# Message passing on sorted edges: register loads once per run, ahead of the clearing matmul

## The chip, the cores and the metric

The kernel runs on one core of one Trainium2 chip. The metric is the device time of one execution in microseconds. The time before the change is 506.3 us, the median of three executions (505.32 to 507.6).

## The reference

4096 nodes have 256 features each, and 262,144 edges have a source and a destination, drawn at random. Each edge carries its source's features, transformed, to its destination, where the messages are summed:

```python
self_out = nodes @ w_self
src_feat = nodes[edges_src]
msg = src_feat @ w_msg
agg = np.zeros((N, D), dtype=np.float32)
np.add.at(agg, edges_dst, msg)
return (self_out + agg).astype(np.float32)
```

## The kernel before

The kernel turns the gather and the scatter into matmuls. In the first 193 us it sorts the edges on VectorE (DVE), with transposes on TensorE (PE), by a key of three parts: a segment of 374 destinations (SW; there are 11, NSEG), a block of 128 sources (NB = 32), and the destination. It also projects all nodes, Y = nodes @ w_msg, in 32 blocks. The sorted edges are cut into 2048 chunks (NCOL) of 128.

The stage after the sort, the run stage, is what the change touches. A run is one pair of segment and source block; there are 11 x 32 = 352 (NRUN), with 5.8 chunks on average. For each run PE builds a matrix of edge counts, 128 sources by 374 destinations plus a spill of 112, in one of six PSUM banks (RING). In program order, the loop over the chunks (lines 422 to 450) does this:

- DVE builds one-hot matrices for 32 chunks at a time, `e` (source within its block) and `d` (destination relative to the chunk's smallest), in four buffers each (line 312).
- `clear(r)` (343 to 350) is a matmul with zeros that opens run r's bank: 224 columns, the two strips where runs overlap. It waits for the eviction of run r - 6, which had the same bank. It is issued nine chunks (MARG) before the run's expected first chunk, `first(r)`.
- For each chunk one matmul (`count_mm`, line 440) adds the one-hot product, 112 columns wide, to the ring at an offset that depends on the data. The offset was computed on DVE into the tile `poff`, 128 rows of 16 values (G16). [...] it must be loaded from `poff` by PE's own instruction stream (lines 430 to 432, eight chunks at a time).
- `evac(r)` (352 to 362): when nine chunks past the run's expected end are done, ScalarE (ACT) copies the bank to SBUF as bf16, into one of 14 buffers of `atr`.
- `merge` (369 to 376): for two of three pairs of runs the spill columns are added into the next run's buffer by an accumulating DMA that GpSimd (POOL) issues. For the others PE does it, with one more matmul (392).
- `apply_run` (378 to 410): some 46 chunks later (LAG), PE multiplies the counts with Y in three matmuls of 256 columns (397) into `out_ps`. At the first run of a segment six matmuls (386) put in nodes @ w_self; at its last, ACT copies the result out and SyncE (SP) stores it.

The order on every engine is the one written here (`manual_schedule`): no scheduler moves anything. Each matmul on PE is two instructions, a weight load (LDWEIGHTS, PEld in the profile) and the matmul proper. The compiled order puts the weight load of the first matmul after a register load ahead of that register load. So before the change the sequence is LDWEIGHTS of a chunk, register load, matmul of that chunk. A wait on another engine sits on the weight load.

Of the kernel before, what the change touches and what calls it, by code (L numbers as in the profile page):

```python
# [20 lines left out]
BW = 512  # L21
SW = 374
W = 112
# [4 lines left out]
RING = 6  # L28
MARG = 9
# [5 lines left out]
PSUM0 = 0x2000000  # L35
# [32 lines left out]
def kernel(  # L68
# [9 lines left out]
    nc = tc.nc  # L78
# [4 lines left out]
    NCOL = E // P  # L83
    assert NCOL == 2048
    T = N // P
    G16 = NCOL // P
# [77 lines left out]
    for h in range(NQ):  # L164
# [3 lines left out]
        c = slice(h * HC, (h + 1) * HC)  # L168
# [24 lines left out]
    end = (NRUN - 1) * SW + N - (NSEG - 1) * SW - SW * OFF  # L193
# [37 lines left out]
    def col16(name, dt):  # L231
        return meta.tile([P, G16], dt, name=name)

    k16, kn, g7f = (col16(n, FP32) for n in ("k16", "kn", "g7f"))
    k16i, kni, rho, rhoc, gi, g7, gn, dl, sl, wr, poff = (
        col16(n, I32)
        for n in ("k16i", "kni", "rho", "rhoc", "gi", "g7", "gn", "dl", "sl", "wr", "poff")
    )
# [66 lines left out]
    def onehots(c, n):  # L305
        res = []
        if c in split_at:
            split_vals(c, split_at[c])
        for nm, val, wid in (("e", slo_b, P), ("d", rel_b, W)):
            o = ohp.tile([P, 16, wid, 2], BF16, name=nm + "_oh", tag=nm, bufs=4)  # L310
            shp = [P, n // 2, wid, 2]
            tt(  # L312
                out=o[:, 0:n // 2],
                in0=val[:, c:c + n].rearrange("p (g i) -> p g i", i=2).unsqueeze(2).to_broadcast(shp),
                in1=jrow[:, 0:wid, :].unsqueeze(1).to_broadcast(shp),
                op=ALU.is_equal,
            )
            res.append(o)
        return res


    def first(r):
        return 187 * r // 32 if r <= NRUN - NB else 1870 + 89 * (r - NRUN + NB) // 16
# [6 lines left out]
    def count_mm(ap, lhsT, rhs, start, after=()):  # L330
        mm = nc.tensor.matmul(  # L331
            out=ap, lhsT=lhsT, rhs=rhs, start=start, stop=True, skip_group_check=True,
        ).ins
        tc.declare_no_dep(
            mm, group="evac", keep=after, reason="disjoint banks by static schedule"
        )
        for i in after:
            tc.add_manual_dep(mm, i.name, DEP, reason="bank free")
        tc.add_to_no_dep_group("count", mm)
        last_mm[0] = mm  # L340
        return mm

    def clear(r):
        b = (r % RING) * BW
        after = [evac_of[r - RING]] if r >= RING else []
        zone = bass.AP(
            tensor=ring.tensor, offset=ring[:, b:b + 1].offset,
            ap=[list(ring[:].ap[0]), [SW, 2], [1, W]],
        )
        count_mm(zone, zer[:, 0, :], zer[:, 1:3, 0:W], True, after)  # L350

    def evac(r):
        at = ats[r % NAT]
        b = (r % RING) * BW
        ins = nc.scalar.copy(out=at[:, 0:SW + W], in_=ring[:, b:b + SW + W]).ins  # L355
        tc.declare_no_dep(
            ins, group="count", keep=[last_mm[0]], reason="disjoint banks by static schedule"
        )
        tc.add_manual_dep(ins, last_mm[0].name, DEP, reason="run complete")
        tc.add_to_no_dep_group("evac", ins)  # L360
        evac_of[r] = ins
        at_of[r] = at
# [3 lines left out]
    def by_dma(r):  # L366
        return r < NRUN - 8 and r // 2 % 3 > 0

    def merge(r):

        i, j = r % NAT, (r + 1) % NAT
        pairs = [(i, j, 2)] if j + 2 <= NAT else [(i, j, 1), (j, 0, 1)]
        for a, b, n in pairs:
            nc.gpsimd.dma_start(  # L374
                out=atr[:, b:b + n, 0:W], in_=atr[:, a:a + n, SW:SW + W], accum_op=ALU.add
            )

    def apply_run(r):
        s, b = divmod(r, NB)
        at = at_of[r]  # L380
        if b == 0:
            for t in range(NT):
                c0 = s * SW + t * P
                m = min(P, N - c0)
                for k in range(2):
                    nc.tensor.matmul(  # L386
                        out=out_ps[0:m, t, :], lhsT=XT[:, k, c0:c0 + m], rhs=wcat[:, k, :],
                        start=(k == 0 and t % 2 == 0), stop=False, skip_group_check=True,
                    )
        spill = at_of.pop(r - 1, None)  # L390
        if r > 0 and not by_dma(r - 1):
            nc.tensor.matmul(  # L392
                out=out_ps[:, 0, :], lhsT=spill[:, SW:SW + P], rhs=Y[:, b, :],
                start=False, stop=False, skip_group_check=True,
            )
        for t in range(NT):
            nc.tensor.matmul(  # L397
                out=out_ps[:, t, :], lhsT=at[:, t * P:(t + 1) * P], rhs=Y[:, b, :],
                start=False, stop=(b == NB - 1), skip_group_check=True,
            )  # L400
        if b == NB - 1:
            o_sb = ohp.tile([P, 3, D], FP32, name="o_sb", tag="o_sb", bufs=2)
            r0, r1 = s * SW, min(s * SW + SW, N)
            nc.scalar.copy(out=o_sb[:, 0:2, :], in_=out_ps[:, 0:2, :])  # L404
            nc.sync.dma_start(
                out[r0:r0 + 2 * P, :].rearrange("(t p) f -> p t f", p=P), o_sb[:, 0:2, :]
            )
            m = r1 - r0 - 2 * P
            nc.scalar.copy(out=o_sb[0:m, 2, :], in_=out_ps[0:m, 2, :])  # L409
            nc.sync.dma_start(out[r0 + 2 * P:r1, :], o_sb[0:m, 2, :])  # L410

    if True:
        todo = []
        regs = []
        ncl = 0
        nev = 0
        starts = {}
        c = 0
        for n in sizes:
            starts[c] = n  # L420
            c += n
        for c in range(NCOL):
            if c in starts:
                c0 = c
                e, d = onehots(c, starts[c])
            ci = c - c0
            while ncl < NRUN and first(ncl) - MARG <= c:
                clear(ncl)
                ncl += 1
            if c % 8 == 0:  # L430
                regs = [nc.tensor.alloc_register(f"po{c}_{i}") for i in range(8)]
                nc.tensor.load(regs, poff[c // G16:c // G16 + 1, c % G16:c % G16 + 8])
            addr = nc.tensor.snap(
                regs[c % 8], donate=True, min_val=PSUM0, max_val=PSUM0 + 4 * (RING * BW - W)
            ).with_bounds(
                min_val=PSUM0, max_val=PSUM0 + 4 * (RING * BW - W),
                guaranteed_mod_val=0, out_of_modulus=4,
            )
            off = (addr - PSUM0) // 4
            count_mm(  # L440
                ring[:, bass.ds(off, W)], e[:, ci // 2, :, ci % 2], d[:, ci // 2, :, ci % 2], False
            )
            while nev < NRUN and (first(nev + 1) - 1 + MARG <= c or c == NCOL - 1):
                evac(nev)
                if nev % 2 == 0 and nev and by_dma(nev - 1):
                    merge(nev - 2)
                todo.append((c + LAG + (SWITCH if nev % NB == 0 else 0), nev))
                nev += 1
            while todo and (todo[0][0] <= c or c == NCOL - 1):
                apply_run(todo.pop(0)[1])  # L450
# [344 lines left out]
```

## Time and profile before

| | |
|---|---|
| median of three executions | 506.3 us |
| the profiled execution, its own time | 506.48 us |
| its span, first to last instruction | 504.5 us |
| PE, DVE, ACT, POOL busy | 355.6, 447.4, 237.9, 158.6 us |
| first and last register load from poff | 194.9 and 492.0 us |
| register loads from poff, of eight registers each | 256 |
| mean granted TensorE clock | 0.916 |

The page cuts the span into 40 slices of 12.6 us and gives each engine's busy share in each, in tenths; the run stage is slices 15 to 39. Each of the costliest groups of instructions has a line: source line, engine, operation, tiles, count, then busy time in all, mean length of one in ns, and the idle time of the engine just before them with what ended most of it. "issue" is a wait that ends with nothing that the profile shows. A matmul's recorded length (213 ns for a chunk) is longer than its distance from the next (51 ns), since matmuls are pipelined. Register loads are not counted as busy; they appear only in the view of their tile or line, under PE's sequencer (PEldq).

### The profile page before, as it was taken

How to read it: one execution, taken by the hardware profiler on the slowest of the kernel's cores; microseconds unless marked ns; L12 is line 12 of the kernel's file. 1: busy time of each engine (PE TensorE's matmuls, PEld its weight loads, DVE VectorE, ACT ScalarE, POOL GpSimd, SP SyncE). 2: the span in 40 equal slices, each digit the busy share in tenths (PEclk: the TensorE clock that was granted, in tenths of full speed). 3: DMA queues.
4: the chain of work that ended last, by engine and by line, in shares of the span. 5: the costliest groups of instructions: out<-in, count | busy, mean ns of one | idle time of the engine just before them, and what ended most of it. 6: DMA issues, size and time to landing. Idle time of an engine off the chain costs nothing. (4 is left out here: it accounts for less than half of the span.)

```text
span 504.5 us, 10056 instructions
## 1 busy us (share of the span) xinstructions
PE 355.6 (70%) x4012; PEld 309.7 (61%) x4017; DVE 447.4 (89%) x403; ACT 237.9 (47%) x452; POOL 158.6 (31%) x154
## 2 busy tenths in 40 slices
PE   0000460766572036899999899999989998989995
PEld 0000430454351015898989789998979898978894
DVE  8999599998899999999999989998979898997810
ACT  3100110121282005476667667676756676765763
POOL 9000000000000000354545345454535554553550
PEclk9999876897897555799999999999999999999999
DMA  8971111110000000133232323333333333332331
GB/s 326 176 185 26 26 26 26 25 26 14 2 0 1 0 0 1 15 29 54 26 53 25 48 28 30 50 28 52 27 51 28 55 26 50 29 55 21 46 37 33
DMA packets 56064, 22.18 MB, mean 44 GB/s; under 512 B 42192, under 2 KB 54992, under 8 KB 56016
## 3 DMA queue, kind: packets, MB, share of 16 engines
q0 software_dynamic: 35920, 8.91, 19.8%
q1 hardware_dynamic: 19520, 10.51, 7.3%
q10 hardware_dynamic: 576, 2.10, 1.1%
q8 instruction: 33, 0.54, 0.5%
q14 instruction: 15, 0.12, 0.1%
HBM read 8.92 MB, written 6.30 MB: 30 GB/s over the span
## 5 line engine op out<-in xcount | busy, mean ns | idle before, releaser
L374 POOL DMA_DIRECT2D atr<-atr x130 | 145.6, 1182 | 331.3 <-ACT atr L355 330.8
L355 ACT CAST atr<-ring 128x486 bf16<-128x486 f32 x352 | 192.1, 566 | 101.3 <-PE ring L331 83.8
L331 PE MATMUL ring<-d_oh,e_oh 128*128 128x112 bf16 x2048 | 181.2, 216 | 14.8 <-issue 8.6
L397 PE MATMUL out_ps<-Y,atr 128*128 128x256 bf16 x1056 | 170.2, 272 | 2.6 <-DMA atr<-atr 2.0
L312 DVE TENSOR_TENSOR e_oh<-slo_b,jrow 128x4096 bf16<-128x4096 int16 (+2 forms) x68 | 147.4, 2167 | 23.4 <-PE ring L331 23.0
L331 PEld LDWEIGHTS <-e_oh 128*128 128x128 bf16 x2048 | 147.3, 99 | 21.1 <-issue 12.9
L312 DVE TENSOR_TENSOR d_oh<-rel_b,jrow 128x3584 bf16<-128x3584 int16 (+2 forms) x68 | 130.1, 1914 | 0.0
L573 DVE TENSOR_TENSOR XA<-XA 128x510 f32<-128x510 f32 (+35 forms) x136 | 92.2, 723 | 11.8 <-ACT XA L699 10.0
L397 PEld LDWEIGHTS <-atr 128*128 128x128 bf16 x1056 | 91.8, 97 | 11.2 <-DMA atr<-atr 2.6
L331 PE MATMUL ring<-zer 128*128 128x224 bf16 x352 | 92.7, 264 | 1.0 <-ACT vals L262 0.7
L695 PE MATMUL tp_sw<-XA,id 128*128 128x128 f32 x192 | 28.0, 308 | 56.3 <-DVE XA L573 56.3
L585 PE MATMUL warm<-zw 128*128 128x512 bf16 x65 | 23.5, 523 | 61.8 <-DVE XA L573 31.9
L695 PEld LDWEIGHTS tp_sw<-XA,id 128*128 128x128 f32 x192 | 26.4, 219 | 59.4 <-issue 57.2
L699 ACT COPY XA<-tp_sw 128x512 f32<-128x512 f32 x24 | 14.2, 591 | 100.6 <-PE tp_sw L695 99.2
L585 PEld LDWEIGHTS <-zw 128*128 128x128 bf16 x70 | 8.2, 125 | 74.4 <-DVE XS L573 29.4
L573 DVE TENSOR_TENSOR XS<-XS 128x512 f32<-128x512 f32 (+17 forms) x40 | 46.0, 1196 | 2.6 <-ACT XS L751 2.0
L331 PEld LDWEIGHTS <-zer 128*128 128x128 bf16 x352 | 34.9, 99 | 4.9 <-issue 0.9
L392 PE MATMUL out_ps<-Y,atr 128*128 128x256 bf16 x123 | 33.4, 272 | 0.0
L262 ACT CAST vals<-tp_sw 128x512 int16<-128x512 f32 x4 | 2.3, 586 | 36.2 <-PE tp_sw L261 36.2
L573 DVE TENSOR_TENSOR XA<-XA,XA 128x62 f32<-128x62 f32 (+7 forms) x16 | 14.7, 919 | 0.3
L392 PEld LDWEIGHTS <-atr 128*128 128x128 bf16 x123 | 11.9, 97 | 2.3 <-issue 2.1
L221 PE MATMUL y_ps<-wcat,XT 128*128 128x256 bf16 x64 | 10.4, 270 | 3.3 <-ACT Y L225 3.3
(81 smaller groups left out, 113.1 us busy)
## 6 DMA issues: line engine op xcount, KB each, us to landing
atr<-atr POOLq DMA_DIRECT2D x98, 56.0 KB, 2.7
out_dram<-o_sb SPq DMA_DIRECT2D x11, 256.0 KB, 3.5
s<-in_edges_src_dram ACTq DMA_DIRECT2D x4, 512.0 KB, 9.5
d<-in_edges_dst_dram SPq DMA_DIRECT2D x4, 512.0 KB
nodes_bf<-in_nodes_dram POOLq DMA_DIRECT2D x1, 2048.0 KB, 16.0
nodes_bf_dram<-nodes_bf SPq DMA_DIRECT2D x1, 2048.0 KB
out_dram<-o_sb SPq DMA_DIRECT2D x10, 118.0 KB
XT<-nodes_bf_dram SPq DMA_TRANSPOSE x64, 2.4
```

The costliest lines, as they stand in the source:

```text
L221: nc.tensor.matmul(out=y_ps[:], lhsT=XT[:, k, t * P:(t + 1) * P], rhs=wcat[:, 2 + k, :], start=(k == 0), stop=(k == 1),)
L262: nc.scalar.copy(out=vals[:].rearrange("p (q k) -> p q k", k=G16)[:, :, 4 * t:4 * t + 4], in_=tp[:].rearrange("p (k q) -> p q k", k=4),)
L312: tt(out=o[:, 0:n // 2], in0=val[:, c:c + n].rearrange("p (g i) -> p g i", i=2).unsqueeze(2).to_broadcast(shp), in1=jrow[:, 0:wid, :].unsq ...
L331: mm = nc.tensor.matmul(out=ap, lhsT=lhsT, rhs=rhs, start=start, stop=True, skip_group_check=True,).ins
L355: ins = nc.scalar.copy(out=at[:, 0:SW + W], in_=ring[:, b:b + SW + W]).ins
L374: nc.gpsimd.dma_start(out=atr[:, b:b + n, 0:W], in_=atr[:, a:a + n, SW:SW + W], accum_op=ALU.add)
L392: nc.tensor.matmul(out=out_ps[:, 0, :], lhsT=spill[:, SW:SW + P], rhs=Y[:, b, :], start=False, stop=False, skip_group_check=True,)
L397: nc.tensor.matmul(out=out_ps[:, t, :], lhsT=at[:, t * P:(t + 1) * P], rhs=Y[:, b, :], start=False, stop=(b == NB - 1), skip_group_check=True,
L573: self.nc.vector.tensor_tensor(out=out, in0=in0, in1=in1, op=op),
L585: ins = self.nc.tensor.matmul(out=w[:], lhsT=self.zw[:, 0:P], rhs=self.zw[:], start=True, stop=True).ins
L695: self.nc.tensor.matmul(out=tp[:, g * P:(g + 1) * P], lhsT=self.turned(rots[8 * h + 4 * t + g]), rhs=sel(x)[:, 4 * t + g], start=True, sto ...
L699: self.nc.scalar.copy(out=sel(y)[:, 4 * t:4 * t + 4], in_=tp[:].rearrange("p (g i b) -> p g i b", g=4, b=bb),)
```

## The change

The registers of a run's chunks are loaded when the run's clear is issued, just ahead of it, up to the chunk at which the next run's clear comes. `regs` becomes a dictionary from chunk to register. [...] where a run crosses a row, or stops one or two chunks short of its end, the load goes to the end of the row, and the rest, if the run needs more, comes with another. The first eight chunks, and the chunks behind the last clear, are loaded where they are used. Nothing else is changed.

```diff
-        regs = []
+        regs = {}
+
+        def load_to(c1):
+
+            c0 = min(c, NCOL) if not regs else max(regs) + 1
+            while c0 < min(c1, NCOL):
+                row = c0 - c0 % G16 + G16
+                end = row if row - c1 <= 2 else c1
+                new = [nc.tensor.alloc_register(f"po{k}") for k in range(c0, end)]
+                nc.tensor.load(new, poff[c0 // G16:c0 // G16 + 1, c0 % G16:c0 % G16 + end - c0])
+                regs.update(zip(range(c0, end), new))
+                c0 = end
+
...
             while ncl < NRUN and first(ncl) - MARG <= c:
+                if c >= 8:
+                    load_to(first(ncl + 1) - MARG)
                 clear(ncl)
                 ncl += 1
-            if c % 8 == 0:
-                regs = [nc.tensor.alloc_register(f"po{c}_{i}") for i in range(8)]
-                nc.tensor.load(regs, poff[c // G16:c // G16 + 1, c % G16:c % G16 + 8])
+            if c not in regs:
+                load_to(c + 8)
             addr = nc.tensor.snap(
-                regs[c % 8], donate=True, min_val=PSUM0, max_val=PSUM0 + 4 * (RING * BW - W)
+                regs.pop(c), donate=True, min_val=PSUM0, max_val=PSUM0 + 4 * (RING * BW - W)
```

In the compiled order the sequence at a clear becomes LDWEIGHTS of zeros, one register load or two in a row, the clearing matmul, LDWEIGHTS and matmul of the next chunk.

## The prediction

> **What bounds the kernel now.** I read the page first: the 40 slices, to find the stage that the change touches, then the cost groups of that stage. The rows used:
>
> ```profile
> PE   0000460766572036899999899999989998989995
> PEclk9999876897897555799999999999999999999999
> L355 ACT CAST atr<-ring 128x486 bf16<-128x486 f32 x352 | 192.1, 566 | 101.3 <-PE ring L331 83.8
> L331 PE MATMUL ring<-d_oh,e_oh 128*128 128x112 bf16 x2048 | 181.2, 216 | 14.8 <-issue 8.6
> L312 DVE TENSOR_TENSOR e_oh<-slo_b,jrow 128x4096 bf16<-128x4096 int16 (+2 forms) x68 | 147.4, 2167 | 23.4 <-PE ring L331 23.0
> L331 PE MATMUL ring<-zer 128*128 128x224 bf16 x352 | 92.7, 264 | 1.0 <-ACT vals L262 0.7
> ```
>
> From slice 16 on PE is at 0.9 or more nearly everywhere, at the full clock. ACT waits 83.8 us for PE, DVE 23.0 us for PE: PE is the bound of this stage, the run stage. Its chunk matmuls (L331, e_oh) idle 14.8 us, most of it before "issue", time for which the page names no releaser. The stage cut in three says the same:
>
> ```profile
> 195.00:260.00 65.00, 60.23 (x742) 55.38 (x742) 65.00 (x38) 41.14 (x78) 28.53 (x26) 0.90 0.27 27
> 260.00:380.00 120.00, 112.71 (x1454) 103.77 (x1454) 111.50 (x58) 78.93 (x150) 60.58 (x55) 1.00 0.35 40
> 380.00:494.00 114.00, 109.15 (x1407) 100.15 (x1407) 91.83 (x48) 77.58 (x146) 56.45 (x51) 1.00 0.34 38
> ```
>
> (PE, PEld, DVE, ACT, POOL busy.) DVE is at 65.00 of 65 at first only because it fills its four buffers; later it waits. The chain of waits covers a few per cent at the end, so it doesn't help here.
>
> The "issue" time belongs to the register loads, which don't count as busy. The views of the tile poff, and of the flag's load at the end:
>
> ```profile
> L432 PEldq TENSOR_LOAD <-poff x256: 586/609/2687, 194.9 to 492.0; - x128
> L480 PEldq TENSOR_LOAD <-flag x1: 490/490/490, 499.3 to 499.3; - x1
> ```
>
> Eight registers take at least 586 ns, one takes 490 on PE: (586-490)/7 = 14 ns a register on a fixed 476 ns. Now what a load waits for. This is the timeline at 229 us:
>
> ```profile
> 228.73 0.56 ACT L355 CAST atr<-ring 128x486 bf16<-128x486 f32 x1 [0.26 <-PE ring L331]
> ...
> 229.78 0.10 PEld L331 LDWEIGHTS <-zer 128*128 128x128 bf16 x1
> 229.89 0.26 PE L331 MATMUL ring<-zer 128*128 128x224 bf16 x1
> 229.89 0.40 PEld L331 LDWEIGHTS <-e_oh 128*128 128x128 bf16 x6
> 229.99 0.42 PE L331 MATMUL ring<-d_oh,e_oh 128*128 128x112 bf16 x5
> ```
>
> ACT's eviction ends at 229.29; the load stands behind the clearing matmul (ring<-zer) that waits for it, starts at 229.3, takes 602 ns and ends at 229.95, 40 ns ahead of its chunk matmul. I laid all instruction records of the trace along PE's program order. Where a load comes right after a clear and its next weight load, 37 of 43 start within 60 ns of the end of the eviction that the clear waits for (median 49 ns). So the sequencer stops at the clear's wait, although that clear reaches the array later. Where a load comes too late, its matmul starts 25 ns after the load's end. The next load starts at least 100 ns after the last one ended.
>
> By the same records 66 places idle because of a load, 16.9 us together. Ten of these hang on loads over 1 us, at the ends of segments, beside the output stores: 8.8 us. 273 us of the stage's 302 are array work, at 51 ns a chunk, 94 a clear and 109 an output matmul.
>
> [...]
>
> **The change part by part.**
>
> Removed: 256 loads of eight, each in front of a chunk matmul, anywhere in its run. Their 16.9 us of idle go. But the 8.8 us beside output stores come back, since a load about every 0.85 us (302 us/352 runs) falls into each of those stores too. Firm gain: 8.1 us.
>
> Added: the order of the built program shows 411 loads with 2048 registers [...]: 291 single ones and 60 pairs, two in a row. 349 of these 351 groups stand between the clear's LDWEIGHTS and the clear's matmul, and 346 of these LDWEIGHTS carry the wait for ACT's eviction of the run six earlier. No DMA, no ACT, DVE or POOL instruction is added or moved; SP's and POOL's queues aren't passed. Queued behind a waiting load on PE is the clear, then its run's chunks; who waits for those is the eviction of the run, so the next clears.
>
> The new lead of a load is what the array has left when the eviction ends. Over all clears the trace gives, from eviction end to clear start, 0.49 us at the tenth percentile, 0.65 median, 1.32 at the ninetieth. A single load of six needs 49 + 476 + 6x14 + 25 = 634 ns; a pair with six needs another 476, 1.11 us. The shortfalls, clear by clear, with the sizes that each clear really gets: singles are short at 145 of 286 clears, 15.6 us in all; pairs at 52 of 60, 23.6 us.
>
> Contention: the old loads under 1 us last on average 56 ns over 586, longer when the spill merges' DMA runs. The new ones meet the same merges: (145 + 2x52) x 0.056 = 13.9 us. Sum 53.1.
>
> Relief: a late clear delays the array, not the evictions that the next one or two clears wait for (their last chunk is 12 chunks, two runs, earlier). So a short pair pays the next single's shortfall (52 x 0.055 = 2.9), and of the other singles about every second pays: (15.6-2.9)/2 = 6.4, and half of their contention, 4.1. 53.1 - 13.4 = 39.7.
>
> The clear moved behind its load costs nothing by itself; 155 more instructions among 8,000 are under 1 us. DVE and ACT get slack. The drain after the last chunk (494 to 499) stays.
>
> Sum: 39.7 - 8.1 = +31.6. The profiled execution took 506.48 us (span 504.5 and 2.0 around it), the median is 506.3: they agree. Forecast 538 us.
>
> Unknown costs, from both sides. Size of a load: 14 ns a register rests on two points; if every load costs 586 whatever its size, the same sums give 19.7 and 30.7, +9 after relief: 547. Below, a single can't be cheaper than the 490 seen. I take 14. Second load of a pair: none stands behind another before, so between nothing (it overlaps) and its full 490 to 590; I take full, since nothing behind a load is seen to start before its end. The clear behind a load: passes or is held; I take held, for the same reason. Output stores: 8.8 us return or not; I take returned.
>
> **Rivals.**
>
> *The clear passes the load.* [...] Against: the stop at a clear's wait shows a sequencer that works in order. It gives 94 ns of cover to each: singles 5.9, pairs 18.9, contention 9.4, relief -5.5, minus 8.1: +20.6, 527 us.
>
> *Pairs overlap.* [...] Singles 15.6, pairs 3.1, contention 9.7, relief -11.8, minus 8.1: +8.5, 515 us. With the clear passing as well: 11.7 - 5 - 8.1 = -1.4, 505 us.
>
> *Faster: the load runs during the clear's wait.* Place: LDWEIGHTS of zer with the wait for ACT. If the weight load waits in its queue, and the sequencer goes on to the register load, the load is done before the clear can go. It decides from the point where a single starts some 0.1 us, and a pair some 0.5 us, before the eviction ends. Price: 8.1 to 16.9 us saved, 494 us in the middle. Against: 37 of 43 loads start right after the eviction. For: there, two instructions stand between wait and load, here none.
>
> *Fewer stalls for fewer late loads.* That the change does no less loading is counted, not argued: 411 against 256.
>
> **How the numbers follow.** Held and in series 0.55 (own range 528 to 550); clear passes 0.15; pairs overlap 0.12; both 0.06; faster 0.07; worse than 556[...], 0.05. About 0.5%, 2.5 us, can be told from no change. Faster: 0.07 and a little of "both", 0.08; same 0.04, from "both"; slower 0.88. The range leaves out "both", "faster" and "worse": 513 to 556.
>
> **What would show it.** The tile poff with 411 loads of about 500 to 600 ns; clears (ring<-zer) idling before "issue", now 1.0 us in all, by 30 us or more, the pairs by 0.4 to 0.5 each; chunks idling less than 14.8; a load starting 50 ns after an eviction, and its clear 25 ns after the load. ACT waits more for PE, DVE too. I am wrong if clears start inside the time of their load, if the second of a pair is much shorter than the first, or if loads start before the eviction ends.

## The result: 798 us, and the profile after

| | before | after |
|---|---|---|
| median | 506.0 us (4 executions) | 797.9 us (4 executions) |
| ratio to before, with its 95% interval | | 1.575 (1.569 to 1.581) |
| span of the profiled execution | 504.5 us | 797.2 us |
| register loads from poff, sum of their time | 256, 181.9 us | 411, 453.5 us |
| mean granted TensorE clock | 0.916 | 0.86 |

Ratios leave out two executions that lie apart from the others of their kernel, one of e6's 22 (1361 us, which nothing here explains) and one of e9's 8 (507.8 us).

The direction was as forecast; the size was nine times what was forecast (+292 us, not +32). The page after, first PE and the clock in 40 slices (now 19.9 us each), then the groups that stood for the stage before:

```profile
PE   0034466505665566656665656666655566565565
PEclk9997698955599997998998987889999989897797
...
L312 DVE TENSOR_TENSOR e_oh<-slo_b,jrow 128x4096 bf16<-128x4096 int16 (+2 forms) x68 | 147.3, 2166 | 301.2 <-PE ring L331 301.2
L355 ACT CAST atr<-ring 128x486 bf16<-128x486 f32 x352 | 193.6, 565 | 387.9 <-PE ring L331 367.8
...
L331 PE MATMUL ring<-d_oh,e_oh 128*128 128x112 bf16 x2048 | 203.1, 229 | 33.0 <-issue 29.8
...
L331 PE MATMUL ring<-zer 128*128 128x224 bf16 x352 | 97.7, 278 | 180.2 <-ACT atr L355 102.6
```

PE stands at 5 or 6 tenths through the whole stage, and DVE and ACT wait for it: DVE 301.2 us (23.0 before), ACT 367.8 (83.8). PE itself idles ahead of the clearing matmuls, 180.2 us against 1.0. The page puts most of that down to ACT's eviction; the timeline below speaks against it. The view of the tile poff shows what grew:

```profile
L423 PEldq TENSOR_LOAD <-poff x411: 313/977/4035, 194.9 to 779.4; - x137
```

The median load takes 977 ns, where it took 609; the shortest 313, where it took 586. Three loads that follow each other, one line for each, cut out of the same view by narrow windows; they carry four registers from column 0 of a row, six from column 4, and six from column 10:

```profile
L423 PEldq TENSOR_LOAD <-poff x1: 350/350/350, 496.7 to 496.7; - x1
L423 PEldq TENSOR_LOAD <-poff x1: 834/834/834, 497.5 to 497.5; - x1
L423 PEldq TENSOR_LOAD <-poff x1: 1479/1479/1479, 498.5 to 498.5; - x1
```

And the timeline of PE and ACT around the last two:

```profile
497.97 0.10 PEld L331 LDWEIGHTS <-zer 128*128 128x128 bf16 x1
498.38 0.26 PE L331 MATMUL ring<-zer 128*128 128x224 bf16 x1
...
499.06 0.10 PEld L331 LDWEIGHTS <-zer 128*128 128x128 bf16 x1
499.35 0.56 ACT L355 CAST atr<-ring 128x486 bf16<-128x486 f32 x1 [0.58 <-ACT atr L355]
...
499.96 0.26 PE L331 MATMUL ring<-zer 128*128 128x224 bf16 x1 [0.69 <-ACT atr L355]
```

The load of 834 ns, from 497.52 in the records, ends at 498.36, and the clear starts at 498.38. The load of 1479 ns, from 498.46, ends at 499.94, and the clear starts at 499.96, 0.9 us after its weight load of 499.06. The wait for the eviction sits on that weight load, so the eviction was over by then: by the records, that of the run six earlier ended at 498.31. "<-ACT atr" is wrong here: the view names a later run's eviction, which ended at 499.91, since a register load isn't among the releasers that it knows.

With each load's first column and length, known from the program, beside its duration, the 411 loads sort like this (medians, ns):

| registers | first column a multiple of 4 | any other first column |
|---|---|---|
| 1 | 316 (22 loads) | |
| 2 | 562 (21) | |
| 3 | 821 (21) | 787 (22) |
| 4 | 347 to 351 (42) | |
| 5 | 601 to 614 (29) | 1247 to 1283 (45) |
| 6 | 850 to 853 (37) | 1510 to 1537 (130) |
| 7 | | 1805 (22) |
| 8 | 615 (18 from column 8) | |

(Two loads are left out: the first eight, 792 ns, and the last nine, 2282.)

A column is 4 bytes. The durations fit this reading, which is an estimate from the table: from a 16-byte boundary a load takes whole fours in one step, and single registers for the rest; from any other place it takes every register in a step of its own. The first step takes about 316 to 350 ns, each further one some 240 to 270. So four registers cost as much as one, and six may cost 850 or 1520. The 191 loads from a boundary brought 814 registers in 116.6 us, 143 ns each; the other 220 brought 1,234 in 337.0 us, 273 ns each. All 256 loads before began on a boundary and had two whole fours. The 586 ns that the prediction read as the least that eight registers take is the price of two such fours; the shortest load here, of one register, takes 313.

### The profile page after: what moved, and what is told of

Its sections match the earlier page's. It is cut to its first block, busy times and chain, and to the rows that moved or that the text cites. A ratio compares the mean times of both kernels' runs of the same rounds, so it can differ in the third digit from the quotient of the medians.

```text
span 797.2 us, 10216 instructions
## 1 busy us (share of the span) xinstructions
PE 444.3 (56%) x4017; PEld 339.6 (43%) x4017; DVE 450.9 (57%) x403; ACT 240.5 (30%) x452; POOL 157.7 (20%) x154
## 5 line engine op out<-in xcount | busy, mean ns | idle before, releaser
L312 DVE TENSOR_TENSOR e_oh<-slo_b,jrow 128x4096 bf16<-128x4096 int16 (+2 forms) x68 | 147.3, 2166 | 301.2 <-PE ring L331 301.2
L355 ACT CAST atr<-ring 128x486 bf16<-128x486 f32 x352 | 193.6, 565 | 387.9 <-PE ring L331 367.8
L331 PEld LDWEIGHTS <-e_oh 128*128 128x128 bf16 x2048 | 154.2, 106 | 268.9 <-issue 259.3
L331 PE MATMUL ring<-d_oh,e_oh 128*128 128x112 bf16 x2048 | 203.1, 229 | 33.0 <-issue 29.8
L397 PE MATMUL out_ps<-Y,atr 128*128 128x256 bf16 x1056 | 196.6, 302 | 10.9 <-issue 10.8
L331 PE MATMUL ring<-zer 128*128 128x224 bf16 x352 | 97.7, 278 | 180.2 <-ACT atr L355 102.6
L397 PEld LDWEIGHTS <-atr 128*128 128x128 bf16 x1056 | 103.7, 108 | 22.9 <-issue 9.3
L331 PEld LDWEIGHTS <-zer 128*128 128x128 bf16 x352 | 37.6, 107 | 10.5 <-issue 3.9
L392 PE MATMUL out_ps<-Y,atr 128*128 128x256 bf16 x123 | 37.7, 307 | 0.0
L386 PE MATMUL out_ps<-wcat,XT 128*128 128x256 bf16 (+1 forms) x66 | 15.0, 393 | 0.0
L392 PEld LDWEIGHTS <-atr 128*128 128x128 bf16 x123 | 13.5, 110 | 0.7
```

Source lines behind the costliest of these rows:

```text
L312: tt(out=o[:, 0:n // 2], in0=val[:, c:c + n].rearrange("p (g i) -> p g i", i=2).unsqueeze(2).to_broadcast(shp), in1=jrow[:, 0:wid, :].unsq ...
L331: mm = nc.tensor.matmul(out=ap, lhsT=lhsT, rhs=rhs, start=start, stop=True, skip_group_check=True,).ins
L386: nc.tensor.matmul(out=out_ps[0:m, t, :], lhsT=XT[:, k, c0:c0 + m], rhs=wcat[:, k, :], start=(k == 0 and t % 2 == 0), stop=False, skip_gro ...
L392: nc.tensor.matmul(out=out_ps[:, 0, :], lhsT=spill[:, SW:SW + P], rhs=Y[:, b, :], start=False, stop=False, skip_group_check=True,)
L397: nc.tensor.matmul(out=out_ps[:, t, :], lhsT=at[:, t * P:(t + 1) * P], rhs=Y[:, b, :], start=False, stop=(b == NB - 1), skip_group_check=True,
```

## The experiments

**e1: only the alignment.** The kernel before; poff stands in a wider tile, one column to the right.

```diff
...
+    poff_w = meta.tile([P, G16 + 8], I32, name="poff")
+    poff = poff_w[:, 1:1 + G16]
...
```

> The kernel before, with poff laid one column (4 bytes) to the right in a wider tile; the same 256 loads of eight at the same places. Theory A (a load whose first value isn't on a 16-byte boundary fetches its registers one by one, some 245 ns each): each load takes about 316 + 7x245 = 2.0 us, and the kernel takes 750 to 800 us with nothing moved. Theory B (it is the place in front of the clear, held and in series, that costs 292 us): loads stay at 609 ns in the median, 506 us.

814.4 us against 505.5 (one execution of it, seven of before):

```profile
L434 PEldq TENSOR_LOAD <-poff x256: 1927/2025/4642, 195.9 to 798.9; - x128
```

The same 256 loads at the same places, none moved or added, now take 2025 ns each in the median, as long as eight steps (316 + 7 x 244): 547 us in all. Four bytes of address cost 309 us, somewhat more than the changed kernel. Theory B falls as the main cause.

**e5: the control, 16 bytes.** The same with `4:4 + G16`.

> As e1, but poff stands four columns (16 bytes) to the right, so that loads of eight begin on a 16-byte boundary and not on one of 32. A with a boundary of 16 bytes: nothing changes, 609 ns in the median and 506 us within 1%. If the wider tile itself cost the 309 us of e1, or the boundary were 32 bytes, it would be near 814 us or between.

504.4 us (one execution), against 506.2:

```profile
L434 PEldq TENSOR_LOAD <-poff x256: 586/607/2366, 195.6 to 489.9; - x128
```

The wider tile costs nothing, and loads of eight that begin 16 bytes further on take 607 ns in the median, where those of before take 609: what counted in e1 is a boundary of 16 bytes, not of 32.

**e2 and e3: only the place.** The changed kernel, its loads cut to aligned eights (e2) or fours (e3):

```diff
             c0 = min(c, NCOL) if not regs else max(regs) + 1
+            c1 = -(-c1 // 8) * 8
             while c0 < min(c1, NCOL):
                 row = c0 - c0 % G16 + G16
-                end = row if row - c1 <= 2 else c1
+                end = min(c0 + 8, row, c1)
```

> The changed kernel, but each load ahead of a clear is rounded up to an aligned eight: 256 loads of eight as before, all in front of clears. A: median load near 609 ns, 500 to 525 us; the place alone costs at most 20 us. B: the place is what costs, so near 798 us.

> The changed kernel with each load rounded up to aligned fours: 512 loads of four, one or two in front of each clear. A: each load near 350 ns, 500 to 535 us. Theory C (the number of loads and pairs in series costs): 512 loads and 160 pairs are more than the 411 and 60 of the changed kernel, so slower than 798 us or near it.

```profile
L424 PEldq TENSOR_LOAD <-poff x256: 586/607/2344, 195.3 to 509.9; - x128
```

e2: 524.9 us, ratio 1.035 (1.028 to 1.041); median load 607 ns, in the line above. e3: 552.0 us, ratio 1.089 (1.082 to 1.095); median load 336 ns. So the place alone costs 19.3 us (524.86 - 505.54), a fifteenth of the change. In e2's records 169 of 251 loads ahead of a clear start within 60 ns of the end of the eviction that the clear waits for, none sooner than 44 ns; idle time that ends with a load ("load-bound" from here on) is 35.2 us where it was 16.9. e3 is slower than theory A said, but with 512 loads and 160 pairs it is 246 us faster than the changed kernel, so it isn't the number of loads or pairs either: theory C falls as the main cause. What e3 takes over e2 lies in its load-bound idle, some 54 us, and in pauses at blocks of instructions, some 16 us (4 in e2; the last section).

**e10: only the price.** The changed kernel's loads, cut at the same odd places, but issued ahead of the last matmul before a clear, so that in PE's order they stand before the clear's wait. The hook, in `apply_run` (or ahead of the chunk's matmul where no run is applied at that chunk):

```diff
...
         for t in range(NT):
+            if ahead is not None and t == NT - 1:
+                load_to(ahead)
             nc.tensor.matmul(
...
```

> The loads of the changed kernel, with its starts and lengths (411, 62 pairs), at the places of e6, ahead of the clear's wait. If the price of the loads is nearly all of the 292 us and the place some 20 to 30 us of it, 740 to 785 us. If the two multiply (a long load hurts only because it begins when the eviction ends), far less: 550 to 700 us.

```profile
L425 PEldq TENSOR_LOAD <-poff x413: 307/1070/3907, 195.9 to 765.8; - x138
```

785.3 us (two executions), ratio 1.551 (1.544 to 1.558); 413 loads with 453.8 us in all. Moving the loads out of the wait gives back 12.6 of 292 us. Without the wait, the price costs 280 (785.3 - 505.3), and at the old price the place costs 19: together 299, near the 292 of both. They add up; they don't multiply. That neither these new places nor the number of loads makes the 280 is shown by the next three runs (505 to 515 us).

**e6, e7, e11: aligned loads ahead of the wait.** The places of e10 with aligned eights, sixteens and fours; for e6:

```diff
...
+        def load_to(c1):
+            while loaded[0] < min(c1, NCOL):
+                k = loaded[0]
+                new = [nc.tensor.alloc_register(f"po{k + i}") for i in range(8)]
+                nc.tensor.load(new, poff[k // G16:k // G16 + 1, k % G16:k % G16 + 8])
+                regs.update(zip(range(k, k + 8), new))
+                loaded[0] = k + 8
...
```

> 256 aligned loads of eight, of the chunks of the next run, issued ahead of the last matmul before a clear, so that the sequencer passes the load before it stops at the clear's wait for the eviction. If the cost of the place in e2 (19 us) is a load that begins only when the eviction ends, then here the loads start earlier and lie in the time in which the sequencer would wait: 490 to 506 us, and less load-bound idle time than the 16.9 us of before. If the place ahead of a clear costs for another reason, near 525 us.

> As e6 with a whole row of poff, sixteen registers, in one load: 128 loads. Price by fours: 336 + 3x264 = 1.13 us each, 145 us in all against 182 of the loads before; 495 to 512 us. If each load had one price whatever its size, about 0.6 us, it would be well below 500 us.

> 512 aligned loads of four at the places of e6. In e4 (fours at use) the load-bound idle rose by only 7 us, and 24 us lay in 18 pauses at the border of a block of 256 instructions, beside a fetch of instructions, where the kernel before has 3.4 us. If such pauses come from the number of loads in a block, they stay near 20 us here, and the kernel takes 515 to 530 us. If they come from a sequencer that is late, because the loads hold it where they are used, they go with the place: 500 to 510 us.

e6: 504.7 us, ratio 0.9973 (0.9957 to 0.9989): faster than before by a quarter of a per cent, and 20 us under e2, which has the same loads. So what costs in e2 is that the load begins only when the eviction ends (none of its 251 sooner than 44 ns after it). Load-bound idle is 15.6 us at 36 places (66 before), and 8.6 of it lies at loads over 1 us, beside the output stores. e7: 515.4 us, ratio 1.017 (1.012 to 1.022), above the expected 495 to 512. Its loads take 1102 ns at least, 1154 in the median, near the 1.13 us that was expected of four steps, but 167.5 us in all, not 145, since 37 of them take over 1.3 us, all 37 beside packets of the merges or the stores (none of the 32 loads without such packets does); 88 of 128 hold PE up. e11: 508.6 us, ratio 1.005 (1.000 to 1.010), not told apart from before.

**e4 and e8: fours and sixteens where they are used.** The kernel before with 4 or 16 in place of 8; for e4:

```diff
-            if c % 8 == 0:
-                regs = [nc.tensor.alloc_register(f"po{c}_{i}") for i in range(8)]
-                nc.tensor.load(regs, poff[c // G16:c // G16 + 1, c % G16:c % G16 + 8])
+            if c % 4 == 0:
+                regs = [nc.tensor.alloc_register(f"po{c}_{i}") for i in range(4)]
+                nc.tensor.load(regs, poff[c // G16:c // G16 + 1, c % G16:c % G16 + 4])
...
```

> The kernel before with loads of four at every fourth chunk in place of eights: 512 loads. A: 350 ns each, shorter than what the array has queued (0.65 us in the median), so most of the 16.9 us of load stalls go: 492 to 508 us. C: twice the loads, slower than 506 by 10 us or more.

> The kernel before with sixteen registers at every sixteenth chunk, where they are used: 128 loads of 1.13 us if the price goes by fours. That is longer than the 0.65 us that the array has left when an eviction ends, so nearly each of them stalls, by about 0.3 us: 520 to 545 us, though the loads take less time in all than before.

e4: 536.2 us, ratio 1.057 (1.049 to 1.065). The 492 to 508 us of theory A were missed. The loads are as cheap as said,

```profile
L432 PEldq TENSOR_LOAD <-poff x512: 326/337/2097, 195.9 to 521.7; - x171
```

but load-bound idle rose to 24.0 us, and 23.7 us of pauses without a load turned up at 18 places (the last section). The time is what theory C said, but its cause, the number of loads, isn't enough: e11 has as many. e8: 541.3 us (one execution), as expected: 109 of its 128 loads hold PE up, 56.8 us, though all loads together take less time (167.2 us) than before (181.9). A shorter sum is no gain here, since each piece (1156 ns in the median) is longer than what the array has left when an eviction ends (0.65 us in the median, in the prediction).

**e9: no loads beside the output stores.** e6, with loads running up to 45 chunks ahead before a segment's store:

```diff
...
+                for q in quiet:
+                    if q - RAMP <= c < q and loaded[0] < q + LEN + 8:
+                        ahead = max(ahead, loaded[0] + 1)
...
```

> As e6, but in the 84 chunks ahead of a segment's output store one aligned eight is loaded at every clear, up to 45 chunks ahead, so that none is loaded for 24 chunks after it. In e6 load-bound idle is still 15.6 us at 36 places, most of it at loads over 1 us beside the stores. If these loads are slow because they run beside the store, loads over 1 us become few (before: 15) and the time falls by 5 to 11 us below e6: 494 to 500 us. If they are slow for another reason at the end of a segment, about 505 us.

503.1 us (8 executions), ratio 0.992 (0.989 to 0.996): the lowest median here, 0.8% under before. Its gain over e6 is 1.6 us between the medians, not the 5 to 11 expected, with intervals that just touch. Loads over 1 us fell from 13 to 7, what they hold up from 8.6 to 3.4 us. In the traces of before, e6 and e9 every load over 1 us (15, 13 and 7) overlaps packets of an output store, and none without such packets reaches 0.9 us: the slow loads are those beside a store, as the prediction said, and e9 keeps not all loads away from it. In the profiled execution of e9 new pauses at instruction blocks (7.2 us against 0.8 in e6) stand against the 4.8 us of load-bound idle that it saves.

## Why the prediction was wrong

*The step that failed: the price of a load.* "Size of a load: 14 ns a register rests on two points": a load of eight (586 ns) and one of a single flag (490 ns), read as 476 ns fixed and 14 ns a register. By the table the eight were two steps of four (347 to 351 ns for one four, 615 for two) and not eight registers; the flag's load, at the end of the kernel, took 490 for a reason that no run shows, and a single register from poff takes 316. A line through these two points has no meaning. With it 411 loads and 2048 registers came to 411 x 0.476 + 2048 x 0.014 = 224 us, 247 with contention; they took 453.5. Six registers, the commonest load, were priced at 560 ns and took 850 in 37 cases and some 1,520 in 130. The bound from both sides didn't save it: it varied the price with the number of registers and never with the address. At the true prices nearly all of the 292 us is there before any place is looked at (e10, 280), so the direction owes little to the sum that forecast it. All 256 loads of the trace had one alignment, so the trace couldn't show its effect, and that was itself the warning. "A single can't be cheaper than the 490 seen" was wrong for the same reason.

*Held at the clear's wait, held behind the load, pairs in series: right, but the wait seldom binds.* In the changed kernel no load begins before its clear's eviction ends (45 ns after it at the earliest, 346 cases), but only 48 begin within 60 ns of it (169 of 251 in e2). 240 begin within 105 ns of the end of the load before (53 in e2): here one load waits for another, not for an eviction. 269 of 349 clears start 24 to 30 ns after their load's end, none sooner; the second of a pair starts 100 ns (median) after the first ends. So neither "the clear passes the load" nor "pairs overlap" holds here.

*Shortfalls and relief: overrun.* The sum, lead by lead, with a late clear paying for the next one, supposes that the sequencer catches up between loads. A load about every 0.76 us (305 us of stage, about 400 loads) that takes 1.1 us on average never lets it. Most of what the loads grow by then becomes idle time: they grew by 271.6 us and load-bound idle by 211, in e1 by 365 and 254. No run has the loads that the prediction priced; the nearest, e2, aligned eights without pairs, takes 19.3 us more than before, where +32 was forecast.

*Costs put at nothing.* "155 more instructions ... are under 1 us" left out the pauses at blocks of instructions (the last section): 16 of them take 42.3 us, 3.4 before. Its pairs got a second 476 ns but not the 100 ns that it had itself read between two loads, some 5 us over its 52 short pairs. And the granted clock fell (0.86 against 0.916, chunk records of 229 ns, not 216): no part of the sum holds that, and everything above 556 us had one chance in twenty. Of the stage's +293 us (304.8 to 597.5), 211 are load-bound idle (227.9 against 16.9) and 39 these pauses; the other 43 are, by estimate, about what the lower clock takes. Chunks follow each other at 51 ns where the trace's clock reads 1.0 and at 94 ns where it reads 0.5; what matmuls without a load or a pause take over their full-clock distance sums to 50 us at 0.5 (4 before) and 1 us at 1.0. Why the clock fell, no run shows.

*The loads beside output stores return: right.* The longest load of the changed kernel took 4.0 us, beside a store; in e9, with fewer loads beside the stores, loads over 1 us fall from 13 to 7, and all 7 overlap one.

*The faster rival* named the right mechanism at the wrong place: the compiled order puts the wait ahead of the load, and in the changed kernel none of 346 loads begins before its clear's eviction ends. Written out by hand, with aligned loads, it gives e6.

*What was to show it:* 411 loads, clears idling by 30 us or more, ACT and DVE waiting for PE came. "About 500 to 600 ns" for a load and "chunks idling less than 14.8" (they idle 33.0) did not, and the first of them is the main error.

## What to carry to other kernels

A price read from one alignment and one size is known for these alone: if a change gives loads other starts or lengths, look for a trace that has them, or measure one, before a line is drawn through two points. As measured here, register loads are best started at a multiple of 16 bytes (six registers took 850 to 853 ns in the median from there, 1510 to 1537 from elsewhere), with whole fours (of four, eight and sixteen, eights did best: 504.7 us, against 508.6 and 515.4), and issued ahead of a wait on the same engine, not behind it (504.7 us in e6, 524.9 in e2). PE's sequencer worked in order in the changed kernel: none of 346 loads began before the eviction had ended that the weight load ahead of it waits for, and no clear sooner than 24 ns after its load. Its own instructions are then a queue with a sum of its own: 411 x 1.1 us was more than the array's work (273 us before, by the prediction's records), and no view of busy engines shows that sum.

## What the runs showed that was not expected

*Pauses at blocks of 256 instructions.* In the changed kernel PE stops for 0.9 to 3.8 us at places that lie a multiple of 256 of its instructions apart, with no load under way, as here at a chunk in the middle of a run:

```profile
464.29 0.26 PE L331 MATMUL ring<-d_oh,e_oh 128*128 128x112 bf16 x2
468.07 0.45 PE L331 MATMUL ring<-d_oh,e_oh 128*128 128x112 bf16 x3 [3.53 <-issue]
```

The DMA queue that the page calls "instruction" (q8, 33 packets of 16 KB) has a packet from 465.77 to 466.69, a fetch from here on. In all, 16 such pauses begin beside a fetch, and PE goes on 2.2 to 3.0 us after the fetch began: 42.3 us, against 4 pauses and 3.4 us before, where at 21 of the 28 such places after 215 us the last fetch began over 4 us before PE got there. e4, with 512 fours where they are used, has 18 and 23.7 us; e11, with as many fours ahead of the wait, 4 and 3.6 us. So it isn't the number of loads alone. Nor is it the place alone: e3, with as many fours at the clear, has 18 pauses and 16 us, e10, with odd loads ahead of the wait, about as much as the changed kernel (42 us), and e1, the slowest of all, none. Why the fetch begins so late is open.

*A gap between two loads.* The next load never starts sooner than 99 ns after the last one's end, in any of these kernels (100 ns before, 99 in the changed kernel), whatever their lengths; what fills the gap isn't shown.
